# Reordering the expert groups of the last mixture-of-experts layer, and mixing lane widths in the rounds that gather rows

## The chip, the core and the metric

The kernel runs on one core of one Trainium2 chip. The metric is the device time of one execution in microseconds (us), the median over runs. The engines that matter here are PE (TensorE: matmuls), DVE (VectorE), ACT (ScalarE) and SyncE (SP), whose queue issues the weight loads by DMA.

## The reference, cut to what matters

A two-layer backbone over 256 latent and 256 context tokens with D = 1024. Each layer ends in a mixture of experts. What the change touches is the one of layer 1, which works on the 256 latent tokens alone:

```
scores = sigmoid(h @ router_w); best of 4 groups by its top-2 biased scores; top-2 experts inside it
w = scores of the two experts, normalised to sum 1
for e in range(16):
    y = y + comb[:, e:e+1] * ((silu(h @ w1[e]) * (h @ w3[e])) @ w2[e])
```

w1 and w3 are 1024x512 per expert, w2 is 512x1024, all float32: 6 MB per expert, 96 MB for the layer.

## The kernel before, in words

The stage is `moe_chip` (line 779 on). `finish` (called at L801) makes the routing: for each token and expert a position in the expert's list (`pos`), a weight (`wts`) and a mask. From the counts the 14 experts other than experts 0 and 1 are ranked by size on DVE (L974 to L982). A *lane* is a place for some rows of one expert, and lanes are worked on in *groups*, mostly pairs (`GROUPS`, L818):

- lanes 0 and 1 are experts 0 and 1 with 64 rows each; their numbers are known when the kernel is written;
- lanes 2 and 3 are both the largest of the others (128 rows, its weights loaded once: the *shared* pair);
- lanes 4 to 8 are the next five, 64 rows each; lane 8 (`LAST`) is worked on alone, at the end;
- lanes 9 to 16 are the eight smallest, 32 rows each; pairs of them are called small.

Rows that don't fit are done in a loop at the end (`further`), which does the same for all data.

For each group in turn (loop at L1127): the up projections (`up` L846, 64 matmuls of 64 columns by 512 for a pair of 64-row lanes; `up_small` L857, 64 matmuls of 32 columns issued side by side through `side_by_side`, L235, for a small pair), SiLU and product on ACT and DVE (`gated`, L866), the sums of the group before (`put_back`, L927, matmuls at L934), the row weights and the matrix of the way back (`way`, L1041; two rows on DVE at L1063 for a small pair), the turn of the gated rows (`a_turn`, L874), the down projection (`down_pair` L885, matmuls at L893; `down_small` L897, matmuls at L235), and the weighting (`weighted`, L918).

The rows of a lane are gathered by matmuls with a one-hot matrix. `pick` (L821) makes that matrix for several lanes with one compare on DVE (L825), and `picked` (L832) yields after each chunk of matmuls (L841) and ACT copy (L843), so that chunks can be set between other work. The first round (lanes 0 and 1) is done at once (L1006). `later` (L1070) lists three more rounds of 4 chunks each: lanes 2 to 5, lanes 9 to 16, lanes 6 to 8. `AHEAD` (L1125) says how many chunks are drawn in each group before and after its down projection. The tiles `oh` and `x` of a round have two buffers each, taken in turn; the first load into an `x` buffer (below) counts as one.

Weights come in tiles of 1 MB from `pass_tiles` (L937), which follows `GROUPS`: per expert four tiles for the up projection and two for the down projection (small pairs half by half, both experts). `wtile` (L127) issues each from SyncE into the next of the ring's slots, 15 in this stage (RING1 6, RINGB 3, RING3 4, RING4 2). The first 12 tiles (lanes 0 and 1) are issued before the ranking, 10 of them into ring slots, one into an `x` buffer and one into the `yh` and `yl` buffers (L961 to L966). From the second group on, `values_load` (L949) reads on SyncE the number of each expert of the group out of `ctl`, ahead of the group's first tile; `ctl` is written by three casts (L990, through `lanes_of`): lane 2, lanes 4 to 8, lanes 9 to 16. A tile whose slot has not been read to the end waits in SyncE's queue, and all later ones behind it.

At the end lane 8's down projection is done in two column halves (L1158 to L1167), added, and the result is written (L1168 to L1176).

Of the kernel before, what the change touches and what calls it, by code (L numbers as in the profile page):

```python
# [8 lines left out]
F32R = mybir.dt.float32r  # L9
I32 = mybir.dt.int32  # L10
AF = mybir.ActivationFunctionType
OP = mybir.AluOpType
# [4 lines left out]
P = 128  # L17
D = 1024
J = D // P
# [11 lines left out]
CAP, HALF = 128, 64  # L31
# [52 lines left out]
def _model(tc, nc, ctx, A, out, dbg):  # L84
    V, SC, PE, GP, SY = nc.vector, nc.scalar, nc.tensor, nc.gpsimd, nc.sync
# [8 lines left out]
    def pt_(shape, tag, dt=F32):  # L94

        return psum.tile(shape, dt, tag=tag, name=tag, bufs=PB[tag])

    def wt_(shape, tag, dt=F32):

        pool = cur["late"] if tag in cur.get("lt", ()) else cur["wk"]  # L100
        return pool.tile(shape, dt, tag=tag, name=tag, bufs=cur["wb"].get(tag, 1))
# [41 lines left out]
    small, at_ = {}, 0  # L143
# [11 lines left out]
    slots = const.tile([P, P], F32, name="slots")  # L155
# [122 lines left out]
    def splitw(w, eng=V):  # L278

        a, b = w.shape[1:] if len(w.shape) == 3 else (1, w.shape[1])  # L280
        both = []
        for tag in ("hi", "lo"):
            t = wt_([P, 1024], tag, F32R)[:, 0:a * b]
            both.append(t.rearrange("p (a b) -> p a b", a=a) if len(w.shape) == 3 else t)
        hi, lo = both
        SC.copy(hi, w)  # L286
        eng.tensor_tensor(lo, w, hi.bitcast(F32), op=OP.subtract)  # L287
        return hi, lo
# [490 lines left out]
    def moe_chip(finish, shift, fst, rt, rowp):  # L779
# [3 lines left out]
        n, nb = S, S // P  # L783
# [17 lines left out]
        pos, wts, msk = finish(rt, put_row, *shift, counts)  # L801
# [8 lines left out]
        QUART = HALF // 2  # L810
        FIX, MED = 2, 5
        DYN = NE - FIX

        LAST = FIX + 1 + MED
        SMALL0 = LAST + 1
        LANES = SMALL0 + DYN - 1 - MED

        GROUPS = [(0, 1), (2, 3), (9, 10), (4, 5), (11, 12), (6, 7), (13, 14), (15, 16), (LAST,)]  # L818
        OH, X = {}, {}

        def pick(ps, cols, width=HALF):  # L821

            m = len(ps)
            oh = wt_([P, nb, 4 * HALF], "oh", F32R)[:, :, 0:m * width].rearrange("p b (l r) -> p b l r", r=width)
            V.tensor_tensor(oh, slots[:, None, None, 0:width].to_broadcast([P, nb, m, width]),  # L825
                            cols.to_broadcast([P, nb, m, width]), op=OP.is_equal)
            x = wt_([P, J, 4 * HALF], "x")[:, :, 0:m * width]
            for i, p in enumerate(ps):
                OH[p], X[p] = (oh, i), x[:, :, i * width:(i + 1) * width]
            yield from picked(oh.rearrange("p b l r -> p b (l r)"), x, m * width)  # L830

        def picked(oh, x, cols):  # L832

            nj = 1 << (512 // cols).bit_length() - 1
            for q in range(J // nj):
                xt = pt_([P, nj, cols], "pj")
                for jj in range(nj):
                    j = nj * q + jj
                    for b in range(nb):
                        for r in (r_hi, r_lo):  # L840
                            PE.matmul(xt[:, jj], lhsT=r[:, b, j * P:(j + 1) * P], rhs=oh[:, b],  # L841
                                      start=(b == 0 and r is r_hi), stop=(b == nb - 1 and r is r_lo))
                SC.copy(x[:, nj * q:nj * q + nj], xt)  # L843
                yield
# [29 lines left out]
        def a_turn(ac):  # L874
            at = pt_([P, 4, HALF], "ad")
            for k in range(4):
                PE.transpose(at[:, k, :], ac[64:128, k * P:(k + 1) * P], ident[64:128, 64:128])
            a = wt_([P, 4, HALF], "at")
            SC.copy(a, at)
            return a  # L880
# [56 lines left out]
        def pass_tiles():  # L937
# [5 lines left out]

            for es in GROUPS:
                es = [e for e in es if e != FIX + 1]
# [46 lines left out]
        pw, pr = R("pw", 2, nb, 32), R("pwr", 2, nb, DYN)  # L992
# [10 lines left out]
        V.tensor_copy(pw[:, 1, :, FIX + 1], pw[:, 1, :, FIX])  # L1003
        V.tensor_scalar(pw[:, 0, :, FIX + 1], pw[:, 0, :, FIX], float(HALF), None, op0=OP.subtract)
        V.tensor_scalar(pw[:, 0], pw[:, 0], 1e3, None, op0=OP.min)
        first = pick(range(FIX), pos[:, :, 0:FIX, None])  # L1006
        for _ in first:
            pass

# [54 lines left out]
                backs.append(back[:, c, :])  # L1064
            return we, backs

        def columns(ps):
            return pw[:, 0, :, ps[0]:ps[-1] + 1][:, :, :, None]

        def later():  # L1070
            for ps, width in ((range(2, 6), HALF), (range(SMALL0, LANES), QUART), (range(6, SMALL0), HALF)):
                yield from pick(ps, columns(ps), width)

        dst = out.rearrange("(j p) t -> p j t", p=P)

# [46 lines left out]
                SY.dma_start(dst, XT[:, :, L:])  # L1122


        AHEAD = [(2, 2), (2, 2), (0, 0), (0, 0), (2, 2)] + [(0, 0)] * 4  # L1125
        picks, prev = later(), None
        for es in GROUPS:  # L1127
            shared, small = FIX in es, es[0] >= SMALL0
# [17 lines left out]
            ats = [a_turn(acs[0])]  # L1146
            before, after = AHEAD.pop(0)
            for _ in range(before):
# [55 lines left out]
    cols = mp.tile([P, 3, NB, 64], F32, name="cols")  # L1204
# [9 lines left out]
    parts = [splitw(w[:, :, 0:P])]  # L1214
    for j in range(J):
# [3 lines left out]
        for m, eng in enumerate((V, GP)):  # L1219
            s = slice(m * L, (m + 1) * L)  # L1220
            a, b = A1[:, j, m:m + 1], B1[:, j, m:m + 1]
# [18 lines left out]
    first = [pt_([P, T], t) for t in ("pj", "o")]  # L1240
# [4 lines left out]
    def proj_fm(w, m, tag="pj"):  # L1245

        hi, lo = splitw(w[:, :, m * P:(m + 1) * P])
        ps = pt_([P, T], tag)
        for k in range(J):
            mm3(ps, hi[:, k, :], lo[:, k, :], h_hi[k], h_lo[k], k == 0, k == J - 1)  # L1250
        return ps
# [32 lines left out]
    for c, r in enumerate((rq, rk)):  # L1284
        quads, sqs = pt_([P, T], "a"), []
        for m in range(4):
            if m % 2 == 0 and (c or m):
                w = wtile(w_in[:, :, c * 512 + m * P:c * 512 + (m + 2) * P], J, 256)
            if c == 0 and m < 2:
                ps = first[m]  # L1290
            else:
                ps = proj_fm(w, m % 2, ("pj", "o")[m % 2])
# [547 lines left out]
    zero = wt_([P, P], "row")  # L1840
    GP.memset(zero, 0.0)
    moe_chip(finish, shift, fst, rt, wk)
    fst.close()
    st.close()
# [62 lines left out]
```

## Time and profile before

| | us |
|---|---|
| median of 3 runs | 1133.13 (1132.81 to 1135.21) |
| the profiled execution's own time | 1136.91 |
| its span, first to last instruction | 1135.1 |
| PE busy in the span | 1033.8 (91%) |
| DVE busy | 677.5 (60%) |
| ACT busy | 511.0 (45%) |
| expert loads in the stage, after the ranking | 84, issued from 885.61 to 1094.2 |

The profile is of one execution. Times in its rows are microseconds from the span's start, unless a row says ns. PE's busy time says that matmuls are under way, not that the engine is at its peak. A matmul's line can be that of a helper: L235 is every matmul issued side by side. [...]

### The profile page before, as it was taken

The numbers are of one execution on the slowest core, as the hardware profiler recorded it, in microseconds if no ns is written. First come the engines' busy times: TensorE is split into PE (matmuls) and PEld (weight loads), VectorE is DVE, ScalarE is ACT, GpSimd is POOL, SyncE is SP. The second block draws the span as 40 slices with busy tenths as digits, with TensorE's granted clock in tenths as the row PEclk, the third lists the DMA queues.
The fourth block names the chain that finished last, engine by engine and source line by source line (L and its number), as shares of the span: only waits on it lengthen the run. The fifth ranks groups of instructions, "written<-read, shape, count | busy, mean of one in ns | idle before, by whom it ended". The sixth has DMA issues, their size and how long they took to land.

```text
span 1135.1 us, 15156 instructions
## 1 busy us (share of the span) xinstructions
PE 1033.8 (91%) x5527; PEld 699.9 (62%) x5527; DVE 677.5 (60%) x1469; ACT 511.0 (45%) x857; POOL 109.9 (10%) x93
## 2 busy tenths in 40 slices
PE   5799999999998399999999999799997999989675
PEld 1577846566775378888888887478765544433213
DVE  3533389556786699999999996755757411111101
ACT  2422254347445168888888884424443111111000
POOL 0300000002000321121212010420001000000000
PEclk9699999999999699999999999899998899989878
DMA  9832246582428489999999978550396796999993
GB/s 374 282 114 83 74 173 226 189 293 75 187 95 349 146 313 374 383 400 383 395 388 385 399 257 292 211 209 1 123 366 253 308 359 258 420 421 419 420 419 125
DMA packets 76926, 310.44 MB, mean 274 GB/s; under 512 B 6192, under 2 KB 27952, under 8 KB 50608
## 3 DMA queue, kind: packets, MB, share of 16 engines
q1 hardware_dynamic: 66000, 290.23, 65.1%
q0 software_dynamic: 4320, 15.73, 5.3%
q10 hardware_dynamic: 6528, 3.47, 1.0%
q8 instruction: 45, 0.74, 0.3%
q14 instruction: 33, 0.27, 0.1%
HBM read 295.78 MB, written 13.63 MB: 273 GB/s over the span
## 4 chain that ended last, share of the span: by engine, by line
PE 81%; DMA 7%; DVE 7%; ACT 2%; issue 1%; POOL 0%; ACTq 0%; DVEq 0%; SPq 0%; POOLq 0%
PE pj L1235 14%; PE o L1235 6%; DMA w<-in_exp_w_dram 5%; PE o L854 5%; PE o L600 5%; PE o L602 5%; PE o L601 5%; PE ad L261 3%; PE o L235 3%; PE t L624 3%; PE t L626 3%; PE t L625 3%; PE o L893 2%; PE a L1330 2%; PE pj L841 1%; PE a L235 1%
## 5 line engine op out<-in xcount | busy, mean ns | idle before, releaser
L287 DVE TENSOR_TENSOR lo<-w,hi 128x1024 fp32r<-128x1024 f32 (+2 forms) x266 | 295.8, 1128 | 44.3 <-ACT hi L286 38.4
L286 ACT CAST hi<-w 128x1024 fp32r<-128x1024 f32 (+2 forms) x268 | 259.9, 973 | 123.2 <-PE o L1235 37.8
L600 PE MATMUL o<-hi,xh 128*128 128x512 f32 x256 | 101.9, 398 | 0.1
L602 PE MATMUL o<-hi,xl 128*128 128x512 f32 x256 | 100.9, 394 | 0.5 <-DVE xl L588 0.5
L601 PE MATMUL o<-lo,xh 128*128 128x512 f32 x256 | 101.0, 395 | 0.0
L871 DVE TENSOR_TENSOR ac<-ac,o 64x512 f32<-64x512 f32 x13 | 9.0, 691 | 115.0 <-ACT ac L870 114.9
L854 PE MATMUL o<-w,x 128*64 128x512 f32 x280 | 66.5, 595 | 0.0
L870 ACT ACTIVATE ac<-o 64x512 f32<-64x512 f32 x13 | 7.7, 589 | 113.8 <-PE o L854 68.4
L602 PEld LDWEIGHTS o<-hi,xl 128*128 128x128 f32 x256 | 48.5, 189 | 11.1 <-DVE xl L588 1.1
L600 PEld LDWEIGHTS o<-hi,xh 128*128 128x128 f32 x256 | 48.5, 190 | 10.3 <-ACT xh L587 0.6
L601 PEld LDWEIGHTS o<-lo,xh 128*128 128x128 f32 x256 | 48.6, 190 | 9.8
L261 PE MATMUL ad<-w,sl 128*32 128x512 f32 x320 | 50.8, 615 | 3.5 <-DMA w<-in_ada_w_dram 3.5
L624 PE MATMUL t<-hi,ah 128*128 128x512 f32 x128 | 53.3, 418 | 0.0
L626 PE MATMUL t<-hi,al 128*128 128x512 f32 x128 | 50.6, 396 | 0.0
L625 PE MATMUL t<-lo,ah 128*128 128x512 f32 x128 | 50.5, 395 | 0.0
L1235 PE MATMUL pj<-h_hi,hi 128*128 128x512 f32 x104 | 44.5, 428 | 5.0 <-ACT h_hi L1222 2.6
L235 PE MATMUL o<-w,x 128*32 128x512 f32 x256 | 34.9, 695 | 11.8 <-DMA w<-in_exp_w_dram 11.8
L854 PEld LDWEIGHTS o<-w,x 128*64 128x64 f32 x280 | 20.5, 137 | 39.0 <-issue 38.0
L1235 PE MATMUL pj<-h_hi,lo 128*128 128x512 f32 x104 | 44.4, 427 | 0.2 <-DVE lo L287 0.2
L1235 PE MATMUL pj<-h_lo,hi 128*128 128x512 f32 x104 | 44.2, 425 | 0.0
L570 POOL DMA_INDIRECT yacc<-ys,idx x14 | 22.1, 1578 | 202.7 <-ACT ys L632 202.7
L924 DVE SCALAR_TENSOR_TENSOR yl<-o,we,yh 128x512 fp32r<-128x512 f32 x12 | 8.9, 749 | 47.7 <-ACT yh L923 47.7
(571 smaller groups left out, 2182.9 us busy)
## 6 DMA issues: line engine op xcount, KB each, us to landing
w<-in_exp_w_dram SPq DMA_DIRECT2D x190, 1024.0 KB, 13.9
w<-in_ada_w_dram SPq DMA_DIRECT2D x48, 1024.0 KB, 8.2
w<-in_even_w_in_dram SPq DMA_DIRECT2D x12, 1024.0 KB, 8.9
w<-in_odd_w_in_dram SPq DMA_DIRECT2D x6, 1024.0 KB, 13.1
XT<-in_xT_dram SPq DMA_DIRECT2D x2, 2048.0 KB
w<-in_even_w_out_dram SPq DMA_DIRECT2D x4, 1024.0 KB
w<-in_odd_w_out_dram SPq DMA_DIRECT2D x4, 1024.0 KB, 8.9
yacc<-jp ACTq DMA_DIRECT2D x5, 512.0 KB, 20.2
```

What stands on the lines that cost most here:

```text
L235: done = PE.matmul(out[32 * q:32 * q + 32, :], lhsT=lhsT, rhs=rhs, start=start, stop=stop)
L261: PE.matmul(ps[32 * q:32 * q + 32, :], lhsT=sl[:, k, :], rhs=w[:, 0, q * 512:(q + 1) * 512], start=(k == 0), stop=(k == J - 1))
L286: SC.copy(hi, w)
L287: eng.tensor_tensor(lo, w, hi.bitcast(F32), op=OP.subtract)
L600: PE.matmul(h_, lhsT=XH[e][:, k, :], rhs=hi[:, i, :], start=(k == 0), stop=False)
L601: PE.matmul(h_, lhsT=XH[e][:, k, :], rhs=lo[:, i, :], start=False, stop=False)
L602: PE.matmul(h_, lhsT=XL[e][:, k, :], rhs=hi[:, i, :], start=False, stop=(k == J - 1))
L624: PE.matmul(yp[c], lhsT=AH[e][:, k, :], rhs=hi[:, s], start=(k == 0), stop=False)
L625: PE.matmul(yp[c], lhsT=AH[e][:, k, :], rhs=lo[:, s], start=False, stop=False)
L626: PE.matmul(yp[c], lhsT=AL[e][:, k, :], rhs=hi[:, s], start=False, stop=(k == 3))
L854: PE.matmul(h[64 * c:64 * c + 64, :], lhsT=x[:, k, :], rhs=ws[c][:, i, :], start=(k == 0), stop=(k == J - 1))
L1235: f = (lambda a, b, **k: PE.matmul(ps, lhsT=b, rhs=a, **k)) if flip else (lambda a, b, **k: PE.matmul(ps, lhsT=a, rhs=b, **k))
```

## The change

The order of the groups becomes (0, 1), (9, 10), (2, 3), (11, 12), (4, 5), (13, 14), (6, 7), (15, 16), (8). Since the small pairs now alternate with the large ones, the rounds of gathered rows are regrouped: lanes 9 to 12 and 2 to 3; lanes 4 to 5 and 13 to 16; lanes 6 to 8. For that `pick` takes several parts, each with a width of its own, and makes one compare for each part into one tile. The chunks of the second round are drawn one by one around the second and third group.

```diff
--- before.py
+++ after.py
@@ -815,19 +815,24 @@
         SMALL0 = LAST + 1
         LANES = SMALL0 + DYN - 1 - MED
 
-        GROUPS = [(0, 1), (2, 3), (9, 10), (4, 5), (11, 12), (6, 7), (13, 14), (15, 16), (LAST,)]
+        GROUPS = [(0, 1), (9, 10), (2, 3), (11, 12), (4, 5), (13, 14), (6, 7), (15, 16), (LAST,)]
         OH, X = {}, {}
 
-        def pick(ps, cols, width=HALF):
-
-            m = len(ps)
-            oh = wt_([P, nb, 4 * HALF], "oh", F32R)[:, :, 0:m * width].rearrange("p b (l r) -> p b l r", r=width)
-            V.tensor_tensor(oh, slots[:, None, None, 0:width].to_broadcast([P, nb, m, width]),
-                            cols.to_broadcast([P, nb, m, width]), op=OP.is_equal)
-            x = wt_([P, J, 4 * HALF], "x")[:, :, 0:m * width]
-            for i, p in enumerate(ps):
-                OH[p], X[p] = (oh, i), x[:, :, i * width:(i + 1) * width]
-            yield from picked(oh.rearrange("p b l r -> p b (l r)"), x, m * width)
+        def pick(src, *parts):
+
+            total = sum(len(ps) * width for ps, width in parts)
+            ohs = wt_([P, nb, 4 * HALF], "oh", F32R)[:, :, 0:total]
+            x = wt_([P, J, 4 * HALF], "x")[:, :, 0:total]
+            at_ = 0
+            for ps, width in parts:
+                m = len(ps)
+                oh = ohs[:, :, at_:at_ + m * width].rearrange("p b (l r) -> p b l r", r=width)
+                V.tensor_tensor(oh, slots[:, None, None, 0:width].to_broadcast([P, nb, m, width]),
+                                src[:, :, ps[0]:ps[-1] + 1, None].to_broadcast([P, nb, m, width]), op=OP.is_equal)
+                for i, p in enumerate(ps):
+                    OH[p], X[p] = (oh, i), x[:, :, at_ + i * width:at_ + (i + 1) * width]
+                at_ += m * width
+            yield from picked(ohs, x, total)
 
         def picked(oh, x, cols):
 
@@ -1003,7 +1008,7 @@
         V.tensor_copy(pw[:, 1, :, FIX + 1], pw[:, 1, :, FIX])
         V.tensor_scalar(pw[:, 0, :, FIX + 1], pw[:, 0, :, FIX], float(HALF), None, op0=OP.subtract)
         V.tensor_scalar(pw[:, 0], pw[:, 0], 1e3, None, op0=OP.min)
-        first = pick(range(FIX), pos[:, :, 0:FIX, None])
+        first = pick(pos, (range(FIX), HALF))
         for _ in first:
             pass
 
@@ -1064,12 +1069,11 @@
                 backs.append(back[:, c, :])
             return we, backs
 
-        def columns(ps):
-            return pw[:, 0, :, ps[0]:ps[-1] + 1][:, :, :, None]
-
         def later():
-            for ps, width in ((range(2, 6), HALF), (range(SMALL0, LANES), QUART), (range(6, SMALL0), HALF)):
-                yield from pick(ps, columns(ps), width)
+            at_ = pw[:, 0]
+            yield from pick(at_, (range(9, 13), QUART), (range(2, 4), HALF))
+            yield from pick(at_, (range(4, 6), HALF), (range(13, 17), QUART))
+            yield from pick(at_, (range(6, SMALL0), HALF))
 
         dst = out.rearrange("(j p) t -> p j t", p=P)
 
@@ -1122,7 +1126,7 @@
                 SY.dma_start(dst, XT[:, :, L:])
 
 
-        AHEAD = [(2, 2), (2, 2), (0, 0), (0, 0), (2, 2)] + [(0, 0)] * 4
+        AHEAD = [(2, 2), (1, 1), (1, 1), (0, 0), (2, 2)] + [(0, 0)] * 4
         picks, prev = later(), None
         for es in GROUPS:
             shared, small = FIX in es, es[0] >= SMALL0
```

## Rows read from the trace of the kernel before

**Rows 1.** The page: its head, and part 4, the chain by engine

```profile
span 1135.1 us, 15156 instructions
...
PE 81%; DMA 7%; DVE 7%; ACT 2%; issue 1%; POOL 0%; ACTq 0%; DVEq 0%; SPq 0%; POOLq 0%
```

**Rows 2.** The chain of waits, its end: start, length, what

```profile
1069.23 19.94 DMA w<-in_exp_w_dram
1089.22 6.20 PE o L235 x32
...
1125.84 1.26 DVE XT L1077 x3
```

**Rows 3.** The engines in three stretches

```profile
890.00:920.00 30.00, 29.32 (x152) 14.35 (x154) 5.92 (x16) 6.14 (x11) 0.00 (x0) 1.00 1.01 422
920.00:960.00 40.00, 39.05 (x254) 17.93 (x250) 5.05 (x11) 6.14 (x11) 0.00 (x0) 1.00 0.70 261
960.00:1090.00 130.00, 106.26 (x661) 43.24 (x665) 15.30 (x34) 12.88 (x24) 0.00 (x0) 0.91 1.01 420
```

**Rows 4.** Waits of SyncE's queue, 885 to 1000: total, times, longest

```profile
SPq L132 <- PE o L893: 23.3, 5, 10.9
```

**Rows 5.** Order of time, SyncE's weight loads: start, length of the issue, what

```profile
885.61 2.90 SPq L132 DMA_DIRECT2D w<-in_exp_w_dram  x5
...
933.97 0.33 SPq L132 DMA_DIRECT2D w<-in_exp_w_dram  x1
...
945.45 0.33 SPq L132 DMA_DIRECT2D w<-in_exp_w_dram  x1
...
953.20 0.33 SPq L132 DMA_DIRECT2D w<-in_exp_w_dram  x1
```

**Rows 6.** Tile w, one load each (D2, D18): issue ns, start; time to landing

```profile
L132 SPq DMA_DIRECT2D w<-in_exp_w_dram x1: 343/343/343, 886.2 to 886.2; - x1
...
DMA to landing us min/median/max: 8.1/8.1/8.1
...
L132 SPq DMA_DIRECT2D w<-in_exp_w_dram x1: 333/333/333, 932.2 to 932.2; - x1
...
DMA to landing us min/median/max: 4.9/4.9/4.9
```

**Rows 7.** Line 949, one group's reads, first and last start; line 990, the casts

```profile
L949 SPq TENSOR_LOAD <-ctl x2: 265/268/271, 894.0 to 894.6; - x2
...
884.35 0.28 DVE L990 CAST ctl<-byrank 1x1 int32<-1x1 f32 x3
```

**Rows 8.** Order of time on DVE: one-hot compares of two sizes

```profile
882.12 0.42 DVE L825 TENSOR_TENSOR oh<-slots,pos 128x256 fp32r<-128x256 f32 x1
...
887.22 0.69 DVE L825 TENSOR_TENSOR oh<-slots,pw 128x512 fp32r<-128x512 f32 x1
```

**Rows 9.** The chain of waits: second to fourth group

```profile
917.01 1.00 PE o L854 x2
...
948.28 0.99 PE o L235 x8
949.28 1.15 PE pj L841 x8
950.42 6.14 PE o L235 x56
...
959.45 0.88 DVE back L1063 x2
...
961.37 5.15 PE o L235 x32
966.51 7.02 PE o L854 x32
...
993.90 0.43 PE a L934 x2
```

**Rows 10.** The engines in one stretch behind (9, 10)

```profile
960.00:965.00 5.00, 4.06 (x24) 1.23 (x28) 0.46 (x2) 0.37 (x1) 0.00 (x0) 0.66 1.02 429
```

## The prediction

> **What bounds the kernel now.** I read the head of the page first, then the chain of waits, then the engines in stretches, and last the queue of SyncE. The profiled execution spans 1135.1 us [rows 1]; with the 1.8 us outside it takes 1136.91 us, 3.8 us above the median 1133.13. I take differences from its trace and subtract them from the median. PE has most of the chain, DMA 7% [rows 1], but that is an average over stages. In the last 50 us the chain waits on expert weights and only from 1089.2 runs on PE to the end [rows 2]: the matmul at 1089.22 is the second half of the up projection of the last small pair (15, 16), released by a load that landed at 1089.17. So the end is that landing plus 45.9 us (1135.1 - 1089.2), and whatever brings it forward brings the end forward.
>
> Then the stretches. Every load here is 1 MB (1024 KB), 2.497 us at the 420 GB/s that hold from 960 to 1090; from 890 to 920 it is 422, but between 920 and 960 only 261, with PE busy 39 of 40 us [rows 3]. That hole is worth 40 x (1 - 261/420) = 15.1 us of transfer. What makes it stands in the queue's waits: up to 10.9 us at one time for the reader of a slot, line 893, a big pair's down projection [rows 4].
>
> I number the 84 loads issued after the ranking D1 to D84. There are 15 slots in the ring (6+3+4+2); 10 hold loads of the first group, so D1 to D5 go out at once [rows 5], and D(n) from D16 on waits until D(n-15) has been read. Before, D1 to D6 are the pair (2, 3), six loads for two lanes' work. D19 goes out at 933.97, D20 waits for D5 of that pair until 945.45, and D22 waits for the first half of (9, 10) until 953.20 [rows 5]. A load alone lands 4.9 us after its issue [rows 6], so nothing moves from about 940 to 946. The hole is PE lagging on a pair that needs much PE for few bytes. Check: D2 landed at 886.2 + 8.1 = 894.3 [rows 6], D74 at 1089.2; 72 loads need 179.8 us and took 194.9, again 15.1 too many.
>
> **The change, part by part.** *Order of the groups.* Bytes and matmuls stay; 12 loads of (9, 10) now stand ahead of the 6 of (2, 3). If DMA never waits, D2 lands at 894.3 and D74 at 1074.1.
>
> *Reads of the expert numbers.* The first group after the ranking now needs two numbers on SyncE instead of one; two such reads start 0.6 us apart, and the second pair's numbers are written by the last of three casts that take 0.28 us together [rows 7]. SyncE's first load waits behind them: +0.7 us (bounds 0.6 and 0.9). All dynamic loads shift, because the DMA is the bound: D2 lands at 895.0, D(n) at 895.0 + 2.497 x (n - 2), D34 at 974.9, D74 at 1074.8. The other 12 reads keep their number and fall where the queue waits anyway.
>
> *One-hot compares.* Five instead of three on DVE: a 128x256 one takes 0.42 us, a 128x512 one 0.69 [rows 8], so each mixed round costs 0.15 more, 0.3 in all. The cover is DVE's long waits for PE; without it 0.3. The count of gather chunks (8 matmuls, 1.15 us [rows 9]) and of ACT copies stays 12 for these rounds. Each mixed round's tile is freed by its last lane: the third round reuses the first one's and is drawn in (4, 5), after (11, 12) has read it. I take nothing.
>
> *Whether PE frees the slots in time.* This decides. PE starts the second group at 917.0 [rows 9], with (9, 10) there. That block took from 948.28 to 966.51, 18.2 us, one chunk within. A second chunk now comes before its down projection: it adds between 0 (in the wait for the two DVE rows at 959.45) and 1.15 us; I take 0.7, so 18.9 and (2, 3) starts at 935.9. That pair took from 917.01 to 947.13 (948.28 less a chunk), 30.1 us with three chunks; now two, 29.0, so (11, 12) starts at 964.9. Its first half is read 4.9 us after its start (953.20 against 948.28 [rows 5, 9]), at 969.8.
>
> Now the slots. D16 needs D1, read at 917.0 + 4.9 = 921.9; to follow without a hole it must be issued 4.9 us before 930.0, so by 925.1. D20 needs the second half of (9, 10), about 925.5, by 935.0. D32 needs a down load of (2, 3), free 1.7 us before the block ends (945.45 against 947.13), at 963.2, by 965.0. D34 needs the first half of (11, 12), at 969.8, by 970.0: 0.2 to spare, the tightest of all. Later: D42 needs a down load of (11, 12), about 981.5, by 990. With PE's durations 0.7 lower or 0.5 higher the hole at D34 is 0 to 0.3 us; I take 0.2.
>
> *PE behind that.* (11, 12) ends at 983.1; (4, 5), 27.4 us (966.51 to 993.90 [rows 9]) with two chunks on top, at 1012.8; (13, 14) with the two others at about 1033; (6, 7) at about 1060. D70, for the first half of (15, 16), lands at 1064.8. So PE is some 5 us early, waits there as before, and the tail of 45.9 us stays.
>
> *Sum.* 15.1 - 0.7 - 0.2 = 14.2 us. 1133.1 - 14.2 = 1118.9, said as **1119**.
>
> [...] After (9, 10) the granted clock was 0.66 for 960 to 965, and its 32 down matmuls took 5.15 us; (4, 5) behind them began at full rate, 32 matmuls in 7.02 us [rows 9, 10]. My block of 18.2 us holds that dip already. [...]
>
> **The rivals.** *Small pair at the low level.* [...] If all of (9, 10), now between PE-bound pairs, runs low: its 64 up matmuls took 0.99 + 6.14 = 7.1 us, while 32 of a late pair took 6.20 [rows 2, 9], so 64 would take up to 12.4: +5.3; the down 5.15 goes to 6.20: +1.1. D34 then goes out 6.4 - 0.2 = 6.2 us late: gain 8.2, 1125. With the first half of (11, 12) low too, 6.20 for 3.6, 2.6 more: 1127.5. For: the dip in rows 10. Against: the up matmuls before it were not slow.
>
> *The hole only moves.* (2, 3) still needs 29 us of PE for six loads, and PE's order need not be that of the source. If the pair's matmuls wait on something not seen (the psum pair that the small group has just used), 12 to 15 us late at D32 to D34, the same hole opens there: 1131 to 1134. Against: PE was busy 39 of the 40 us in which most of that pair ran [rows 3].
>
> *The tail shortens.* If PE comes warm to (15, 16), its second half takes 3.6 instead of 6.20 us: 2.6 less, 1116.3. Against: PE waits some 5 us there, as now.
>
> [...]
>
> **How the numbers follow.** A measurement here tells about 0.2% (2.3 us) from no change. Forecast 0.64, small pair low 0.20, shorter tail 0.05, hole moves 0.06, slower 0.05. Faster: 0.64 + 0.20 + 0.05 = 0.89; same 0.06; slower 0.05. The range goes from the shorter tail, 1116, to both small pairs low, 1127.5; it leaves out the two last, 0.11, and some error of the terms.
>
> **What would show it.** Right: 420 GB/s in every stretch from 890 to 1095 with no hole at 920 to 960; 32-column matmuls from about 917; the last load landed near 1100; the first dynamic issue near 886.3; a chain with a DMA wait that ends near 1075, then the same 46 us. The one-hot compares hidden: no PE wait on DVE above 1 us before a chunk. Wrong: long waits of SyncE for lines 893 or 854 at 960 to 980, a low granted clock at 917 to 965, or PE still at (6, 7) when D74 has landed.

## The result, and the profile after

The changed kernel takes 1118.74 us in the median of 4 runs (1117.72 to 1119.43), the kernel before 1132.97 us (4 runs by now): a ratio of 0.987 with a 95% interval of 0.9852 to 0.9887, which is 14.2 us less (12.8 to 16.8). The forecast was 1119.0. Two executions of the later experiments, at 2051.71 and 3319.63 us, lay far above all others and are left out of what follows.

The head of the page and the chain by engine, and the engines in the same three stretches as [rows 3]. Such a line gives the stretch, its length, for PE, PEld (the weight loads of TensorE), DVE, ACT and POOL the busy time and in brackets the instructions, then the mean granted clock of TensorE as a share of full speed, the busy share of the DMA engines, and GB/s:

```profile
span 1115.9 us, 15166 instructions
...
PE 79%; DMA 8%; DVE 7%; ACT 3%; issue 1%; POOL 0%; ACTq 0%; DVEq 0%; SPq 0%; POOLq 0%
```

```profile
890.00:920.00 30.00, 29.71 (x181) 14.41 (x181) 4.33 (x9) 5.45 (x10) 0.00 (x0) 1.00 1.01 420
920.00:960.00 40.00, 39.52 (x264) 19.81 (x258) 6.27 (x13) 7.11 (x13) 0.00 (x0) 1.00 1.01 420
960.00:1090.00 130.00, 109.32 (x707) 43.90 (x700) 16.56 (x36) 13.52 (x26) 0.00 (x0) 0.96 1.01 420
```

The middle line answers to the hole: 420 GB/s where there were 261. PE is as busy as before, 39.5 of 40 us, but the loads no longer wait for it.

The chain (start, length, what), from the stage's first up matmul on. In the kernel before that matmul began at 889.98.

```profile
887.90 13.88 PE o L859 x64
...
914.35 1.00 PE o L235 x8
...
927.59 3.57 PE o L235 x32
931.16 0.78 PE pj L846 x5
931.94 13.88 PE o L859 x64
...
959.68 3.57 PE o L235 x32
...
1052.51 21.25 DMA w<-in_exp_w_dram
1073.76 0.04 issue
1073.80 6.03 PE o L235 x32
...
1082.14 1.92 PE o L235 x16
...
1100.37 3.70 PE o L1167 x32
```

L235 is now the small pair (9, 10) at 914.35, L859 at 931.94 is (2, 3), and 959.68 is (11, 12). D74 lands at 1073.76, where [rows 2] have 1089.17. The spans of the two profiled executions differ by 19.2 us, in three parts. The stage begins 2.1 earlier (887.9 for 890.0). From there to D74 it takes 185.9 for 199.2 us, 13.3 less: from D2 to D74 the loads take 180.8 for 194.9 us, 14.1 less (the hole, but for about 1 us by which a late load sets it back, see the last section), and D1 goes out 0.8 closer to that first matmul. The tail from D74 to the end is 42.1 for 45.9 us, 3.8 less. The medians differ by 14.2, because the execution of the kernel before that was profiled first lay 3.9 above its median, and the one after 1.0 below.

### The profile page after: what moved, and what is told of

Its sections match the earlier page's. It is cut to its first block, busy times and chain, and to the rows that moved or that the text cites. A ratio compares the mean times of both kernels' runs of the same rounds, so it can differ in the third digit from the quotient of the medians.

```text
span 1115.9 us, 15166 instructions
## 1 busy us (share of the span) xinstructions
PE 1021.4 (92%) x5527; PEld 696.1 (62%) x5527; DVE 677.6 (61%) x1471; ACT 510.5 (46%) x857; POOL 111.0 (10%) x93
## 4 chain that ended last, share of the span: by engine, by line
PE 79%; DMA 8%; DVE 7%; ACT 3%; issue 1%; POOL 0%; ACTq 0%; DVEq 0%; SPq 0%; POOLq 0%
PE pj L1239 13%; PE o L1239 6%; PE o L600 5%; PE o L602 5%; PE o L601 5%; DMA w<-in_exp_w_dram 5%; PE o L859 5%; PE o L235 3%; PE ad L261 3%; PE t L624 3%; PE t L626 3%; PE t L625 3%; PE o L898 2%; PE a L1334 2%; DMA XT<-in_xT_dram 2%; DMA w<-in_ada_w_dram 2%
## 5 line engine op out<-in xcount | busy, mean ns | idle before, releaser
L859 PE MATMUL o<-w,x 128*64 128x512 f32 x280 | 67.8, 596 | 0.0
L859 PEld LDWEIGHTS o<-w,x 128*64 128x64 f32 x280 | 20.6, 137 | 37.9 <-issue 36.3
L235 PE MATMUL o<-w,x 128*32 128x512 f32 x256 | 31.2, 634 | 6.9 <-DMA w<-in_exp_w_dram 6.9
L565 POOL DMA_INDIRECT xg<-rows,idx x16 | 31.5, 1969 | 37.8 <-DVE we L553 17.3
```

Source lines behind the costliest of these rows:

```text
L235: done = PE.matmul(out[32 * q:32 * q + 32, :], lhsT=lhsT, rhs=rhs, start=start, stop=stop)
L859: PE.matmul(h[64 * c:64 * c + 64, :], lhsT=x[:, k, :], rhs=ws[c][:, i, :], start=(k == 0), stop=(k == J - 1))
```

## The experiments

They ran on three chips, so each is compared by its ratio to the kernel before on the same chip. Spread there was up to 8.4 us for the kernel before, so for small differences the transfers in the trace decide.

**The kernel before, again.** No edit.

> The kernel before, unchanged, for a second trace. Theory (the hole in the weight transfers): between 920 and 960 us near 261 GB/s again, a hole of about 15 us of transfer, whatever this execution's total. Rival (the tail did it): in the first trace 45.9 us lie between the landing of the last up load of the pair (15, 16) and the end, in the changed kernel's 42.1 us; if that belongs to the order, the second trace shows 45.9 again; if it is the draw of the clock in one execution, about 42 us, and the execution is some 3 us shorter.

It took 1139.08 us. The engines at the stage's start and in the stretch of the hole:

```profile
885.00:890.00 5.00, 4.71 (x23) 4.23 (x23) 4.50 (x18) 0.84 (x2) 0.00 (x0) 0.50 0.90 372
890.00:895.00 5.00, 5.00 (x16) 1.80 (x17) 0.00 (x0) 0.58 (x1) 0.00 (x0) 0.50 1.03 429
...
920.00:960.00 40.00, 39.82 (x238) 17.53 (x238) 4.09 (x8) 6.96 (x13) 0.00 (x0) 1.00 0.66 240
```

The hole is there and larger. PE was granted 0.50 until 895, where the first trace has 1.00 from 890 [rows 3]; transfers went on meanwhile. By the shortfall against 420 GB/s over 180 us from the stage's start the hole is 20.0 us here and 14.9 in the first trace. So when PE is late, the old order pays. The tail was 45.2 us: long again, which left the draw of the clock open.

**Mixed rounds without the new order.**

```diff
-GROUPS = [(0, 1), (9, 10), (2, 3), (11, 12), (4, 5), (13, 14), (6, 7), (15, 16), (LAST,)]
+GROUPS = [(0, 1), (2, 3), (9, 10), (4, 5), (11, 12), (6, 7), (13, 14), (15, 16), (LAST,)]
```

> The mixed rounds and the new way of drawing chunks, but the old order of the groups. Theory (order of the loads): the hole stays, less one or two chunks of 1.15 us that no longer stand inside the pair (2, 3): about 1131.5 us (1130.5 to 1133). Rival (the regrouped rounds shorten PE's path by themselves): near 1119 to 1125.

1129.57 us against 1133.77, ratio 0.9967 (0.9954 to 0.998): 3.7 us less by the ratio, where 1.5 were expected and the range went to 2.5. The stretch of the hole, shifted by the 3.7 us that this execution's stage began earlier:

```profile
916.00:956.00 40.00, 39.52 (x271) 19.83 (x271) 5.52 (x12) 5.92 (x11) 0.00 (x0) 1.00 0.80 301
```

The hole stays, 40 x (1 - 301/420) = 11.3 us. Fewer chunks stand before the slots of (2, 3) and of the first half of (9, 10) come free, so PE is less late: the regrouped rounds are worth 3 to 4 us in the old order. That is not the 14.

**The new order without mixed rounds.** The old `pick` and rounds; lanes 2 to 5 and 9 to 16 both in the first group.

```diff
-GROUPS = [(0, 1), (2, 3), (9, 10), (4, 5), (11, 12), (6, 7), (13, 14), (15, 16), (LAST,)]
+GROUPS = [(0, 1), (9, 10), (2, 3), (11, 12), (4, 5), (13, 14), (6, 7), (15, 16), (LAST,)]
...
-AHEAD = [(2, 2), (2, 2), (0, 0), (0, 0), (2, 2)] + [(0, 0)] * 4
+AHEAD = [(4, 4), (0, 0), (0, 0), (0, 0), (0, 0), (2, 2)] + [(0, 0)] * 3
```

> The new order with the old unmixed rounds: lanes 2 to 5 and 9 to 16 both gathered in the first group (8 chunks there), lanes 6 to 8 in the sixth. Theory: 8 chunks are done before the pair (11, 12) in either case, so the load that is tightest is not later; (9, 10) starts 4.6 us later, where the loads behind it have 3.7 us to spare: hole of about 0.9 us, 1119.6 us (1118.5 to 1121). Rival (the mixing carries the gain): 1123 (4.6 us later throughout) or more.

1120.53 us, ratio 0.9878 (0.9861 to 0.9896), as expected. The order alone brings nearly all. But the trace's hole is larger than the 0.9 us worked out:

```profile
920.00:960.00 40.00, 36.95 (x257) 16.84 (x258) 4.88 (x12) 5.76 (x11) 0.00 (x0) 0.97 0.93 380
```

That is 40 x (1 - 380/420) = 3.8 us, in an execution of 1123.70 us; the other three took 1119.70 to 1120.57, so their hole was probably smaller. The chain shows why, around the start of (9, 10):

```profile
918.60 1.15 PE pj L841 x8
919.75 0.71 PE a L934 x6
...
920.49 1.22 PE pj L841 x8
921.70 0.99 PE o L235 x8
922.70 1.15 PE pj L841 x8
923.84 0.99 PE o L235 x8
924.84 1.15 PE pj L841 x8
925.98 5.29 PE o L235 x48
```

The chunks stand apart, with other matmuls of PE's order between them. The load D16 went out 38.0 us after the stage's first up matmul, in the changed kernel 31.4: four chunks made it 6.6 us later, 1.65 each instead of 1.15. Mixing the rounds saves this; what it is worth in time is small (1120.53 us here against 1117.82 in the next run, on the same chip).

**Only the first exchange.** Mixed rounds, and behind (2, 3) the old order.

```diff
-GROUPS = [(0, 1), (9, 10), (2, 3), (11, 12), (4, 5), (13, 14), (6, 7), (15, 16), (LAST,)]
+GROUPS = [(0, 1), (9, 10), (2, 3), (4, 5), (11, 12), (6, 7), (13, 14), (15, 16), (LAST,)]
```

> The mixed rounds, and of the new order only the first exchange: (0, 1), (9, 10), (2, 3), (4, 5), (11, 12), (6, 7), (13, 14), (15, 16), (8). Theory: the hole came from (2, 3) standing second; the loads that wait for slots of (4, 5) have about 2 to 4 us to spare, so no hole: 1118.7 us (1118 to 1120). Rival (the alternation through the whole stage is needed, the hole moves to (4, 5)): 1124 to 1131, with a hole near 970 to 990.

1117.82 us, ratio 0.9861 (0.9834 to 0.9887): the same as the whole change, and no hole in its trace.

```profile
920.00:960.00 40.00, 39.51 (x260) 19.71 (x254) 6.17 (x13) 6.85 (x13) 0.00 (x0) 1.00 1.01 419
960.00:1090.00 130.00, 109.39 (x707) 44.62 (x703) 16.75 (x37) 13.81 (x26) 0.00 (x0) 0.96 1.01 420
```

So the place of the shared pair is what counts; alternating behind it adds nothing that shows here.

**Thirteen slots instead of fifteen,** in the changed kernel and in the one before.

```diff
-RING4=2
+RING4=0
```

> The changed kernel with 13 slots in the ring instead of 15. Theory (slots set when a load may start): worked out from the times at which its trace frees the slots, D11 would be 0.4 us late and D14 1.3 us late, the others in time: 1118.7 + 1.5 = 1120.2 us (1119 to 1122). Rival (PE's order, not the slots, made the difference): 1118.7. Rival (two slots are 5 us of transfer in any order): 1123.7.

> The kernel before with 13 slots instead of 15. Theory: the waits for the slots of the pair (2, 3) come two loads earlier, so D20 lands when D22 did: two loads of 2.5 us more, 1133.0 + 5.0 = 1138.0 us (1136.5 to 1139.5). Rival (PE bound, the slots don't matter): 1133.

The changed kernel took 1121.09 us in the median of three executions, ratio 0.9889 (0.9845 to 0.9934), which can't be told from 0.987, so the trace has to decide. It has two slow spots ahead of 920 (909 to 911 and 917 to 919, 287 GB/s in each) and none behind:

```profile
890.00:920.00 30.00, 29.72 (x190) 14.14 (x186) 4.33 (x9) 5.45 (x10) 0.00 (x0) 1.00 1.00 392
920.00:960.00 40.00, 39.51 (x264) 20.02 (x264) 6.27 (x13) 7.18 (x13) 0.00 (x0) 1.00 1.01 421
```

30 x (1 - 392/420) = 2.0 us, worked out as 1.7. The kernel before with 13 slots took 1135.56 us against 1134.28, ratio 1.0017 (0.9994 to 1.004): 1138 was missed. Its hole is what was expected (shown 4 us earlier than in [rows 3], as the stage began 4 us earlier):

```profile
916.00:956.00 40.00, 38.81 (x252) 17.78 (x248) 5.29 (x11) 6.14 (x11) 0.00 (x0) 1.00 0.64 239
```

Over 180 us from the stage's start the hole is 19.9 us, 5.0 more than in the first trace; from the first up matmul to D74 the stage takes 204.0 us instead of 199.2. But its tail took 41.6 us instead of 45.9: in this execution the gap came back there. It was the fastest of the ten (1133.21 us), and the tails of the others are not on record. So the slots set the hole; the total does not show it.

**More work for PE** in the second group, in both kernels.

```diff
             for _ in range(before):
                 next(picks)
+            if es == GROUPS[1]:
+                idle = pt_([P, 2, S], "pj")
+                for i in range(64):
+                    PE.matmul(idle[:, i % 2], lhsT=r_hi[:, 0, 0:P], rhs=posT, start=True, stop=True)
+                SC.copy(nothing, idle[:, 1, 0:1])
```

> The changed kernel with 64 more matmuls on PE (128x256, result not used) in the second group, there (9, 10), ahead of its down projection: at 0.115 us each about 7.4 us of PE. Theory (DMA sets the end, PE has 4.6 us to spare at the load that waits for the first half of (11, 12)): 7.4 - 4.6 = 2.8 us more, 1121.5 us (1120.5 to 1123). Rival (PE sets the end): all 7.4, 1126. Rival (PE has far more to spare): 1118.7.

> The kernel before with the same 64 more matmuls in its second group, there (2, 3), ahead of its down projection. Theory: the hole is PE's lateness on this pair, nothing to spare, so all of it is paid: 1133.0 + 7.4 = 1140.4 us (1139 to 1141.5). Rival (the loads set the end and PE is covered): 1133 to 1135.

In order of time on PE the addition took 7.9 us in the changed kernel, a little above the estimate:

```profile
925.67 7.94 PE L1157 MATMUL pj<-posT,r_hi 128*128 128x256 f32 x64
```

That kernel took 1120.32 us, ratio 0.9872 (0.9838 to 0.9907): not slower beyond its interval, which is too wide to tell the 2.8 us of the theory from nothing. The execution in the trace took 1122.61 us. In it D34 goes out at 969.4 and lands 5.3 us later, at 974.8; counted from D2 it lands 2.7 us later than in the changed kernel, where 2.8 were expected. So some 5 of the 7.9 us of PE's lateness are free there. By D74 the transfers are 4.5 us late. The stretches below 420 GB/s are three:

```profile
961.00:966.00 5.00, 5.00 (x29) 2.74 (x29) 1.30 (x2) 1.51 (x3) 0.00 (x0) 1.00 0.67 239
969.00:972.00 3.00, 3.00 (x29) 1.94 (x29) 0.00 (x0) 0.00 (x0) 0.00 (x0) 1.00 0.81 235
1020.00:1034.00 14.00, 13.20 (x95) 5.07 (x91) 1.50 (x2) 1.90 (x3) 0.00 (x0) 1.00 0.99 380
```

They lose 2.2, 1.3 and 1.3 us. Ahead of the first SyncE waits until 963.0 for a down projection (D32), ahead of the second until 969.5 for the first half of (11, 12) (D34). In the third come waits for a down projection and for a small pair, until 1019.6 and 1030.0, which the theory had not reckoned with. The kernel before with the same addition took 1138.27 us against 1134.28, ratio 1.0032 (1.0014 to 1.0049): 3.6 us more by the ratio, under the 7.4 expected, though its hole has grown to 22.8 us, 7.9 more than 14.9. It stands here:

```profile
917.00:965.00 48.00, 47.60 (x320) 25.71 (x316) 4.51 (x9) 6.62 (x13) 0.00 (x0) 1.00 0.59 219
```

Its tail, too, was shorter by 3.7 us (42.2). So the hole takes PE's lateness one for one in the old order, and the time shows half of it (3.6 of 7.9 us).

**One read ahead of D1 instead of two.** Each number is read ahead of its expert's own first load.

```diff
+                if p >= FIX and p not in ex:
+                    c = nx + 1 + p
+                    ex[p] = nc.values_load(ctl[0:1, c:c + 1], engines=[mybir.EngineType.SP], min_val=0, max_val=NE - 1)
                 return w[p] if p < FIX else w[bass.ds(ex[p], 1)].rearrange("o p j f -> p (o j) f")
...
-                for e in es:
-                    if e >= FIX:
-                        c = nx + 1 + e
-                        ex[e] = nc.values_load(ctl[0:1, c:c + 1], engines=[mybir.EngineType.SP], min_val=0, max_val=NE - 1)
```

> The changed kernel, but each expert's number is read just ahead of its own first load, so that D1 waits for one read instead of two. Theory (the second read ahead of D1 shifts all loads by 0.6 us, and DMA sets the end): D1 goes out some 4.1 us ahead of the stage's first up matmul instead of 3.5, time 0.6 us less, 1118.1 against 1118.7; that is less than the interval will be, so the trace decides. Rival (the reads are hidden): D1 as before. Risk: the second number's read now stands between D2 and D3, 0.6 us that the loads in flight cover.

1119.1 us, ratio 0.987 (0.9836 to 0.9904): no difference that can be measured. Line 949, its first two reads, and D1 with the loads behind it:

```profile
L949 SPq TENSOR_LOAD <-ctl x2: 270/280/289, 880.7 to 882.9; - x2
...
881.84 8.08 SPq L132 DMA_DIRECT2D w<-in_exp_w_dram  x6
```

D1 goes out 1.1 us after the first read starts; in the changed kernel the reads start at 882.6 and 883.5 and D1 goes out at 884.30, 1.7 after the first. The 0.6 us are real, but the total can't show them: the interval is wider, and the tail of this execution is 46.1 us, 4.0 longer. The two places, from its chain:

```profile
1080.00 3.52 PE o L235 x16
...
1099.83 5.38 PE o L1166 x32
```

**Both kernels again.** No edit.

> The changed kernel, unchanged, for a second trace. If the length of the tail is the draw of the clock in each execution, two stretches of 1.6 us (the first half of the last small pair's down projection, and lane 8's down projection) are each at one level or the other: 42 to 46 us from the landing of D74 to the end. If the short tail belongs to this kernel: 42.2 again.

> The kernel before, unchanged, for a third trace. Hole of 15 to 20 us again; the more of it, the longer PE stays at the low clock as the stage begins. Tail: 45 to 46 us if the long tail belongs to this kernel, anywhere from 42 to 46 if it is a draw.

The changed kernel took 1115.94 us with a tail of 42.4, the one before 1135.77 us with a tail of 45.8. The stretch of the hole, first in the kernel before, then in the changed one:

```profile
920.00:960.00 40.00, 38.57 (x254) 17.93 (x250) 5.52 (x12) 6.14 (x11) 0.00 (x0) 1.00 0.70 262
```

```profile
920.00:960.00 40.00, 39.51 (x264) 19.94 (x264) 6.27 (x13) 7.19 (x13) 0.00 (x0) 1.00 1.01 420
```

So 261, 240 and 262 GB/s in three traces before, and no hole in either trace after. From the first up matmul to D74 the stage took 199.2, 201.4 and 198.9 us before, 185.9 and 186.1 after. The tails do not look like a plain draw (three of three long before, two of two short after), though five traces can't exclude one, and they do not follow the order (short in two kernels with the old order, long in one with the new).

## Why the prediction was right, step by step

**The hole and what made it: right.** The stage was bound by the transfer of weights, with 15.1 us of it lost because PE freed the slots of the pair (2, 3) late. With the pair in third place the shortfall is gone, and D2 to D74 took 180.8 us (892.98 to 1073.76) for 179.8 worked out. The slot and delay runs show the mechanism in both orders. From the trace, D2 and then D34, its start and the time to landing:

```profile
L132 SPq DMA_DIRECT2D w<-in_exp_w_dram x1: 343/343/343, 884.9 to 884.9; - x1
DMA to landing us min/median/max: 8.1/8.1/8.1
...
L132 SPq DMA_DIRECT2D w<-in_exp_w_dram x1: 333/333/333, 963.3 to 963.3; - x1
DMA to landing us min/median/max: 9.4/9.4/9.4
```

One reading of the prediction needs care: it took a long wait of SyncE for line 893 as what makes the hole. The changed kernel waits for the same line, now 898, nearly as long:

```profile
SPq L132 <- PE o L898: 18.0, 4, 8.4
```

The longest of these ends at 956.6, in a stretch at 420 GB/s: enough loads were in flight. A wait alone is no hole; what counts is whether the load goes out early enough.

**The second read: right.** +0.7 was said; 0.6 was measured, and taking it away moved D1 by as much.

**The compares: right.** PE's chain waits for no 128x256 compare, and the two of a round each took 0.42 us. It does wait 0.56 us for the third round's 128x384 compare, as in the kernel before.

**The time that PE has to spare: right in sign, wrong in size.** The step "0.2 to spare, the tightest of all" was mis-sized: D34 went out at 963.29 and landed at 972.74, in step with its neighbours, so with 4.9 us for a load alone [rows 6] it had 972.7 - 4.9 - 963.3 = 4.5 us to spare. Three terms were too long. (9, 10) took 17.6 us (914.35 to 931.94), not 18.9: its 32 down matmuls took 3.57 us, not the 5.15 of [rows 9], at a granted clock of 1.00 where [rows 10] have 0.66. That 5.15 was no fixed cost of this group: in the second trace of the kernel before the same 32 took 3.64, in the third 5.13, and in the old order with mixed rounds 3.57, at a granted clock of 1.00 from 955 to 960. (2, 3) took 27.7 (to 959.68), not 29.0: the chunk that is gone from its up projection had cost 1.0 us more than its own 1.15. In the kernel before two of the 64 matmuls took 1.00 us ahead of it [rows 9], and behind it

```profile
919.16 13.88 PE o L854 x62
```

while all 64 in one run now take 13.88. The first half of (11, 12) was read after 3.6, not 4.9, as no chunk stood in it. All of these erred the same way, and the result did not depend on them, since the bound was met: the 0.2 of the sum came out as 0.

**PE behind that: right.** The last load of the chain starts at 1052.51 and PE waits for it.

**The tail of 45.9 us that "stays": wrong in this trace.** It took 42.1. The two places are in the chain above: 16 down matmuls of (15, 16) in 1.92 us and lane 8's 32 in 3.70; in the kernel before, 3.52 and 5.38:

```profile
1097.73 3.52 PE o L235 x16
...
1117.56 5.38 PE o L1163 x32
```

The rival of a shorter tail had put it at the wrong place: the second up half at 1073.80 was slow in both (6.03 and 6.20 us). How many of the timed runs of each kernel had which tail can't be seen, so how much of the 14.2 us is tail stays open; the gain from the stage's start to D74 alone, 13.3 us, lies within the interval. That the median met the forecast to 0.3 us is partly luck: a late load that was not foreseen (about 1 us, last section) and a tail that was said to stay and did not enter the measured time with opposite signs.

**The rivals.** A small pair at the low level: fell, the granted clock is 1.00 from 920 to 960. A slower kernel, given 0.05: that was the author's estimate for (2, 3) at a low granted clock, and this trace does not show one there. At 931.94 its 64 up matmuls ran in 13.88 us at 1.00, as those of (0, 1) did at 887.90. Behind the chain's last DMA wait the clock was lower: the 32 up matmuls at 1073.80 took 6.03 us at a granted clock of 0.62, against 3.57 at 1.00 for the 32 at 959.68. Around the first two mixed pairs, from 890 to 960, it is 1.00 throughout. The hole that only moves: fell, each of the three stretches stands at 420 GB/s.

## What to carry to other kernels

When a stage streams weights through a ring of slots and both PE and DMA are nearly full, look at the order of the groups by their ratio of PE time to bytes. Here a group with much work for few bytes, (2, 3) with 30.1 us of PE for six loads of 2.5 us, held the transfers up when it stood second (261 GB/s from 920 to 960), and with a light one ahead of it, (9, 10) with 17.6 us for twelve, they ran on at 420. Work out for each waiting load when its slot comes free and when it must be issued; the smallest difference is the slack. One exchange was enough here (1117.82 us). To prove it, lengthen PE's work by a known amount in both orders, and compare the transfers in the trace rather than the total alone.

## What the runs showed that was not expected

The tail, the same instructions in the same order, took 41.6 to 46.1 us in these traces. It depends on two groups of down matmuls, each either at 1.9 or 3.5 us and at 3.7 or 5.4 us. In two traces the granted clock (the third number from the end) of these groups shows the difference: in the kernel before,

```profile
1097.70:1101.30 3.60, 3.57 (x20) 0.73 (x22) 0.00 (x0) 0.00 (x0) 0.00 (x0) 0.54 1.02 419
1117.50:1123.00 5.50, 5.44 (x33) 3.17 (x34) 0.48 (x1) 0.52 (x3) 0.00 (x0) 0.69 0.00 0
```

and in the changed kernel

```profile
1082.10:1084.10 2.00, 1.96 (x20) 0.53 (x20) 0.00 (x0) 0.00 (x0) 0.00 (x0) 1.00 0.99 414
1100.30:1104.10 3.80, 3.73 (x33) 2.34 (x34) 0.48 (x1) 0.50 (x3) 0.00 (x0) 1.00 0.00 0
```

So the long tail of the first goes with a granted clock of 0.54 and 0.69 in these groups, the short one with 1.00 in both. It came out long in all traces of the kernel before, in the old order with mixed rounds (45.4) and in the changed kernel with D1 moved 0.6 us earlier; short in the changed kernel, with the first exchange alone (42.2), and in the old order with 13 slots or with more work for PE; and between (43.3 to 43.6), with the second group alone slow, in three variants of the changed kernel. Why the clock falls there in one execution and not in another was not settled. It can hide an effect of 4 us on the total, as in the two runs that added 5 and 8 us to the hole.

In the changed kernel's trace the stream of loads has one slow step: D68 and D69 landed 3.9 us apart instead of 2.5, and D74, in flight then, took 21.3 us from its issue, where the loads issued from 1030 to 1038 took 19.8 to 19.9, about eight times 2.5. It accounts for the 1 us between 180.8 and 179.8. The traces of the changed kernel's second execution, of the first exchange alone and of the single read have such a step too, 3.7 to 4.0 us at D68 or D69. The stretch from 1055 to 1065 still moved 418 to 419 GB/s, so the transfers did not stop: the bytes went to other loads in flight. What delayed this one is not known.
